# A decoder block on one core: two attention results in another PSUM pool, and three left operands of the last product prepared six steps ahead

## The chip, the cores and the metric

The kernel runs on one core of one Trainium2 chip. A core has a matrix engine (TensorE, PE in the profile), a vector engine (VectorE, DVE), an engine for activations and scaled copies (ScalarE, ACT), a general engine (GpSimd, POOL), and a queue that issues most transfers (SyncE, SP). Each runs its own list of instructions in order, and they wait for one another by semaphores. PE writes its results to PSUM, a small memory of banks that DVE and ACT can read. The metric is the time of one execution on the device, in microseconds.

## What is computed

One layer over 1024 tokens of width 1024, all in float32:

```python
def reference(x, ...):
    h = x
    h = h + 0.5 * swiglu(rms_norm(h, ffn1_norm), w1, w3, w2)       # width 2816
    u = rms_norm(h, mix_norm)
    proj = u @ w_in                                                # q | k | v | p | gates
    y_attn = dilated_mixture_attention(q, k, v) @ w_branch_attn    # 3 groups of 4 heads
    y_pool = multiscale_pool(pz, pool_w, pool_scale) @ w_branch_pool
    h = h + (gates[0] * y_attn + gates[1] * y_pool) @ w_out
    h = h + 0.5 * swiglu(rms_norm(h, ffn2_norm), w1, w3, w2)
    return rms_norm(h, final_norm)
```

In the attention each of the three groups has its own window and dilation; the group results of a head are added with weights that come from their softmax denominators.

## The kernel before

**Numbers in two parts.** Each float32 operand of a product is split into a high part, which ACT rounds off, and a low part, which DVE or POOL gets by subtracting the high part from the source. A product is then three matmuls: high by high, high by low, low by high. Large products are done as a scheme of seven block products in the place of eight, so sums and differences of blocks stand in front of the splits.

**The order of the work** is written out by hand: inside `tc.manual_schedule()` each engine runs its instructions in the order of the program text, and the tile framework only adds the waits. A tile is taken from a pool by its tag; each tag has a fixed number of places that are used in turn, and a new tile waits until the readers of the one that had its place before are done. PSUM has two tags of four places each, "mm" and "acc".

**The end of attention** (lines 1909 to 1943). The attention runs over 24 pairs of blocks, `q` from 0 to 23. For each pair `scores` makes the scores, DVE adds the mask (`masked`, line 1649), ACT takes exponents, `trans_p` has PE transpose them (`tp`), and `split_p` splits them into `ehi` (ACT) and `elo` (DVE, line 1693). `values(q)` has PE multiply them with the values, 12 matmuls of 256 columns into a PSUM place named `o` (line 1711), and `gather(q)` has DVE copy that to its rows in SBUF (line 1734). `next(fill)` places a piece of four matmuls of the pooling branch (`yp`, line 1770) between, so that PE has work while others prepare; two products of that branch, `yp14` and `yp15`, are still under way here. `scores` and the factor rows take "mm" places; `tp`, `o` and `yp` take "acc" places.

After the last pair come the factors of the second half of the heads: DVE computes `w` and `f` (lines 1582 to 1590), ACT and DVE spread them to `f_of` (lines 1598 and 1600, ACT for the first and third group), PE transposes them to `fa` (line 1609, "mm"), DVE multiplies the gathered rows with `fa` (line 1743), adds the three groups, with POOL (line 1745), and `att` is split by ACT and DVE (lines 1750 and 1751). Then `merge` has PE multiply `att` with the branch weights (`ya`, line 1836, "mm").

**The last product** (`Down`, lines 714 to 864). The down projection of each feed-forward half is seven products (`DOWN`) of six steps each (`PAIRS`), 42 steps, numbered 0 to 41; the name `f2` marks the second feed-forward half, with which the program ends. A step has a left operand, a block that was written to DRAM earlier, loaded by `load` as `g`, and a right operand, a weight block `raw` or the sum of two (`s_f2w`, line 790). `begin(i)` splits the right one into `bhi` and `blo` and the left one into `ahi` and `alo`, and frees weight blocks that are done with. `multiply` issues 24 matmuls of 512 columns for a step of two blocks (four groups of rows, six each) and 12 for the sixth step of a product, which has one block. `add` has DVE add a finished PSUM place to the rows `h` (`h_last`, line 820).

While step `i` is multiplied, the left operand of step `i + 3` is loaded and step `i + 2` is split. `split` gives the low part to DVE, or, for every fourth split outside the ends, to POOL, in halves of 512 columns:

```python
            self.n_lo += 1
            eng = gp if self.n_lo % 4 == 0 and 1 < n < self.last_shared else ve
```

`g` takes one of three places named `tmp`; `ahi`, `alo`, `bhi` and `blo` have three places each.

During steps 30 to 33 the first four rows of blocks are finished (`after2`, `norm_rows`): ACT squares a row, DVE and POOL get the scale (`nst`, lines 278 and 279), DVE writes the scaled row (`hn`, line 282), and SP sends it to DRAM (line 2234). In the last two steps, 40 and 41, the matmuls are ordered by row group: nine of a group, then its addition, then the end of the norm for the group's rows, which ACT, DVE and POOL share, and the transfers out.

## Time and profile before

| what | value |
|---|---|
| time, median of 3 runs (lowest to highest) | 1894.78 us (1894.72 to 1895.08) |
| the profiled execution, its own time | 1894.76 us |
| its span, first to last instruction | 1893.0 us |
| mean granted clock of TensorE | 0.999 |
| PE busy | 1880.3 us, 99% of the span |
| DVE, ACT, POOL busy | 1334.7, 773.2 and 713.3 us |

A row of the order of time has the start in microseconds from the span's start, the duration, the engine, the source line, the operation with its output and inputs (buffer numbers left out), the shapes, how many equal ones follow each other, and in brackets how long the engine had idled and what ended that. A row of waits has who waited for whom, the total, the number of times and the longest. A row of stretches has the busy time (and the number) of PE, PE's weight loads, DVE, ACT and POOL in it, PE's granted clock, the share of the DMA engines that was busy, and the rate in GB/s. Matmuls overlap: each is listed with some 0.39 us, but they start 0.23 us apart. Of PE's 12.7 us that are not busy, 7.8 lie behind the last matmul, at 1885.2.

### The profile page before, as it was taken

What the parts mean: (1) busy time and instruction counts of PE and PEld (TensorE: products, weight loads), DVE (VectorE), ACT (ScalarE), POOL (GpSimd) and SP (SyncE); (2) the same over time, 40 slices, a digit from 0 to 9 for tenths busy, and PEclk for the clock granted to TensorE, in tenths of its full rate; (3) what the DMA queues carried; (4) which work ended last, traced back from release to release, by engine and by line L of the source; (5) the groups of instructions that cost most, each with busy time, mean ns of one, the idle gap of its engine ahead of it and who ended that gap; (6) DMA issues with size and microseconds to landing.
All of it is one profiled execution on the core that took longest, in us unless ns stands there. A gap on an engine that the chain in (4) does not pass through costs nothing.

```text
span 1893.0 us, 24691 instructions
## 1 busy us (share of the span) xinstructions
PE 1880.3 (99%) x8822; PEld 1562.5 (83%) x8822; DVE 1334.7 (71%) x1975; ACT 773.2 (41%) x1394; POOL 713.3 (38%) x533
## 2 busy tenths in 40 slices
PE   9999999999999999999999999999999999999998
PEld 8888888888888888888888888888888888888886
DVE  6776556557786776657885896887665566577867
ACT  7423333333334543334445772363333333334344
POOL 4433333331223354444555457543333333312221
PEclk9999999999999999999999999999999999999999
DMA  5154223336566526765678868644332223354654
GB/s 191 60 196 167 84 89 108 138 113 214 169 227 207 183 86 210 234 223 195 214 244 314 322 222 287 266 151 153 141 126 99 88 102 118 132 197 157 224 194 145
DMA packets 144019, 330.79 MB, mean 175 GB/s; under 512 B 17560, under 2 KB 39064, under 8 KB 142360
## 3 DMA queue, kind: packets, MB, share of 16 engines
q1 hardware_dynamic: 140152, 318.36, 48.8%
q10 hardware_dynamic: 3744, 10.85, 1.6%
q8 instruction: 70, 1.15, 0.3%
q14 instruction: 53, 0.43, 0.1%
HBM read 229.61 MB, written 99.55 MB: 174 GB/s over the span
## 4 chain that ended last, share of the span: by engine, by line
PE 55%; DVE 2%; ACT 2%; issue 1%; POOL 0%; DMA 0%; ACTq 0%; SPq 0%; DVEq 0%; POOLq 0%
PE u_mixm L331 15%; PE d_f L815 8%; PE wo L2025 4%; PE yp L1770 2%; PE ya L1836 1%; PE o L1711 1%; PE u_f20b L331 1%; PE u_f21a L331 1%; PE u_f210b L331 1%; PE u_f210a L331 1%; PE u_f29b L331 1%; PE u_f29a L331 1%; PE u_f28b L331 1%; PE u_f28a L331 1%; PE u_f27b L331 1%; PE u_f27a L331 1%
## 5 line engine op out<-in xcount | busy, mean ns | idle before, releaser
L815 PE MATMUL d_f<-bhi_f,ahi_f 128*128 128x512 f32 x616 | 240.2, 390 | 0.0
L815 PE MATMUL d_f<-bhi_f,alo_f 128*128 128x512 f32 x616 | 239.8, 389 | 0.0
L815 PE MATMUL d_f<-blo_f,ahi_f 128*128 128x512 f32 x616 | 239.7, 389 | 0.0
L772 POOL TENSOR_TENSOR alo_f<-g_f,ahi_f 128x512 fp32r<-128x512 f32 x60 | 87.2, 1470 | 268.7 <-ACT ahi_f L768 268.7
L331 PE MATMUL u_mixm<-xhi_t_mix,wc_mixm 128*128 128x512 f32 x608 | 157.3, 391 | 0.1
L815 PEld LDWEIGHTS d_f<-bhi_f,ahi_f 128*128 128x128 f32 x616 | 115.7, 188 | 24.3 <-ACT h L415 0.4
L815 PEld LDWEIGHTS d_f<-bhi_f,alo_f 128*128 128x128 f32 x616 | 115.6, 188 | 24.2 <-DVE alo_f L772 0.4
L815 PEld LDWEIGHTS d_f<-blo_f,ahi_f 128*128 128x128 f32 x616 | 115.7, 188 | 23.9
L331 PEld LDWEIGHTS u_mixm<-xhi_t_mix,wc_mixm 128*128 128x128 f32 x608 | 113.5, 188 | 23.9 <-ACT wc_mixm L319 0.6
L331 PE MATMUL u_mixm<-xhi_b_mix,wc_mixm 128*128 128x512 f32 x456 | 120.4, 392 | 0.0
L322 POOL TENSOR_TENSOR wc_mixm<-s_mixm,wc_mixm 128x512 fp32r<-128x512 f32 x52 | 76.9, 1479 | 104.5 <-ACT wc_mixm L319 104.5
L331 PEld LDWEIGHTS u_mixm<-xhi_b_mix,wc_mixm 128*128 128x128 f32 x456 | 84.9, 188 | 17.5 <-issue 0.3
L319 ACT ACTIVATE wc_mixm<-s_mixm 128x512 fp32r<-128x512 f32 x76 | 47.0, 628 | 111.0 <-DVE s_mixm L373 54.0
L768 ACT ACTIVATE ahi_f<-g_f 128x1024 fp32r<-128x1024 f32 x84 | 81.9, 975 | 6.6 <-DMA g_f<-gs_f 6.6
L331 PE MATMUL u_mixm<-xlo_t_mix,wc_mixm 128*128 128x512 f32 x304 | 81.3, 389 | 0.0
L322 POOL TENSOR_TENSOR wc_mixm<-raw,wc_mixm 128x512 fp32r<-128x512 f32 x40 | 60.2, 1507 | 39.7 <-ACT wc_mixm L319 32.3
L2025 PE MATMUL wo<-w_o,o_hi 128*128 128x512 f32 x224 | 69.2, 391 | 0.0
L768 ACT ACTIVATE bhi_f<-s_f2w 128x512 fp32r<-128x512 f32 x55 | 32.9, 628 | 85.7 <-DVE s_f2w L790 67.0
L768 ACT ACTIVATE bhi_f<-s_f1w 128x512 fp32r<-128x512 f32 x55 | 33.0, 629 | 83.4 <-DVE s_f1w L790 70.1
L331 PEld LDWEIGHTS u_mixm<-xlo_t_mix,wc_mixm 128*128 128x128 f32 x304 | 57.1, 188 | 12.0
L772 DVE TENSOR_TENSOR alo_f<-g_f,ahi_f 128x1024 fp32r<-128x1024 f32 (+1 forms) x48 | 58.7, 1223 | 10.3 <-ACT ahi_f L768 10.3
L331 PE MATMUL u_mixm<-xlo_b_mix,wc_mixm 128*128 128x512 f32 x228 | 61.0, 389 | 0.0
(1332 smaller groups left out, 4754.5 us busy)
## 6 DMA issues: line engine op xcount, KB each, us to landing
g_f<-gs_f SPq DMA_DIRECT2D x70, 512.0 KB
gs_f<-y_f SPq DMA_DIRECT2D x88, 256.0 KB
raw<-in_w2a_dram SPq DMA_DIRECT2D x35, 512.0 KB
raw<-in_w2b_dram SPq DMA_DIRECT2D x35, 512.0 KB
gs_f<-gb_f SPq DMA_DIRECT2D x46, 256.0 KB
raw<-in_w1a_dram SPq DMA_DIRECT2D x22, 512.0 KB
raw<-in_w3a_dram SPq DMA_DIRECT2D x22, 512.0 KB
raw<-in_w1b_dram SPq DMA_DIRECT2D x22, 512.0 KB
```

The source lines that it names most:

```text
L319: ac.activation(w[:, 0], src, AF.Copy)
L322: eng.tensor_tensor(w[:, 1], src, w[:, 0].bitcast(F32), op=OP.subtract)
L331: pe.matmul(p, a, b, start=(start and n == 0), stop=(n == 11), skip_group_check=not start)
L768: ac.activation(hi[:, c], src, AF.Copy)
L772: eng.tensor_tensor(lo[:, d], src[:, o], hi[:, d].bitcast(F32), op=OP.subtract)
L815: pe.matmul(self.banks[m][t], l, r, start=(first and q == 0), stop=(last and q == 2))
L1711: pe.matmul(p, l, r, start=(j == 0), stop=(j == end))
L1770: pe.matmul(p, a, b, start=(j == 0), stop=(j == 11))
L1836: pe.matmul(p, a, b, start=(j == 0), stop=(j == 5))
L2025: pe.matmul(banks[m][t], l, r, start=(st == 0 and j == 0 and q == 0), stop=(st == 1 and j == 1 and q == 2))
```

## The change

Two places are changed; everything before 1130 us of the profile stands in the same order as before.

At the end of attention the last two results, `o22` and `o23`, take "mm" places; the split of the last pair is put ahead of the gathering of `o21`; and one piece of filling is moved from the first round of the final loop to the place ahead of it.

In the last product of the second feed-forward half, the left operands of steps 38, 39 and 40 are loaded seven steps ahead and split six steps ahead. They have two places of their own (`ge`), their low parts all go to POOL, and the rings of `ahi` and `alo` have six places.

```diff
@@ Down
+            self.early = range(len(self.steps) - 4, len(self.steps) - 1) if name == "f2" else ()
+            self.lefts = {}
...
         def split(self, side, srcs, n):
+            bufs = 6 if side == "a" and self.early else 3
...
-            self.n_lo += 1
-            eng = gp if self.n_lo % 4 == 0 and 1 < n < self.last_shared else ve
+            if side == "a" and n in self.early:
+                eng = gp
+            else:
+                self.n_lo += 1
+                eng = gp if self.n_lo % 4 == 0 and 1 < n < self.last_shared else ve
...
-            self.ops[i] = (self.split("a", [self.g.pop(i)], i), w)
+            if i not in self.lefts:
+                self.left(i)
+            self.ops[i] = (self.lefts.pop(i), w)
+
+        def left(self, i):
+            self.lefts[i] = self.split("a", [self.g.pop(i)], i)
+
+        def early_g(self, name):
+            return self.dp.tile([P, 1024], F32, tag="ge", bufs=2, name=name)
...
-                if i + 3 < n:
+                if i + 3 < n and i + 3 not in self.early:
                     self.load(i + 3)
+                if i + 7 in self.early:
+                    self.load(i + 7, self.early_g)
...
                 if i + 2 < n and not ahead:
                     self.begin(i + 2)
+                if i + 6 in self.early:
+                    self.left(i + 6)
@@ attention
-    def values(q):
-        both = outs[q] = bank("acc", f"o{q}")
+    def values(q, tag="acc"):
+        both = outs[q] = bank(tag, f"o{q}")
...
-        values(q - 2)
+        values(q - 2, "mm")
+        advance(splits[q - 1], 2)
         gather(q - 3)
-        advance(splits[q - 1], 2)
         advance(factors[1], 2)
         next(fill, None)
         end_branches()
-        values(q - 1)
+        values(q - 1, "mm")
         gather(q - 2)
         gather(q - 1)
+        next(fill, None)
         for n in range(8):
             advance(combines[1][n // 4])
-            if n not in (3, 5, 7):
+            if n not in (0, 3, 5, 7):
                 next(fill, None)
```

DVE's order behind the last pair, before (a name's first number is the pair, `o21` or `elo23`):

```order
L1582 TENSOR_TENSOR w1_10262<-top1_10261,stats1_8679 128x48
L1734 COPY o1_0_10208<-o21_10195 64x256 x2
L1693 TENSOR_TENSOR elo23_10288<-tp23_0_10251,ehi23_10287 128x512
L1693 TENSOR_TENSOR elo23_10288<-tp23_1_10252,ehi23_10287 128x512
L1586 TENSOR_TENSOR f1_10263<-w1_10262,stats1_8679 128x48
```

And now:

```order
L1600 TENSOR_TENSOR w1_10262<-top1_10261,stats1_8679 128x48
L1711 TENSOR_TENSOR elo23_10286<-tp23_0_10251,ehi23_10285 128x512
L1711 TENSOR_TENSOR elo23_10286<-tp23_1_10252,ehi23_10285 128x512
L1752 COPY o1_0_10208<-o21_10195 64x256 x2
L1604 TENSOR_TENSOR f1_10263<-w1_10262,stats1_8679 128x48
```

The copies of `o21` moved from ahead of the two subtractions to behind them; `f`, which follows both, stands where it stood.

PE's order at the same place, before, behind the matmuls of `o23`:

```order
L1609 MATMUL fa1_0_0_10324<-ident_70,f_of1_10299 128x128 x4
L1770 MATMUL yp14_10267<-xhi_t2_mix_5476,wab7_10015 128x512
L1770 MATMUL yp14_10267<-xlo_t2_mix_5477,wab7_10015 128x512 x3
L1609 MATMUL fa1_1_0_10335<-ident_70,f_of1_10299 128x128 x4
L1770 MATMUL yp15_10342<-xhi_b11_mix_3604,wab7_10015 128x512 x3
```

And now:

```order
L1788 MATMUL yp14_10267<-xhi_t2_mix_5476,wab7_10015 128x512
L1788 MATMUL yp14_10267<-xlo_t2_mix_5477,wab7_10015 128x512 x3
L1627 MATMUL fa1_0_0_10328<-ident_70,f_of1_10299 128x128 x4
L1627 MATMUL fa1_1_0_10335<-ident_70,f_of1_10299 128x128 x4
L1788 MATMUL yp15_10342<-xhi_b11_mix_3604,wab7_10015 128x512 x3
```

Four matmuls of the filling stand ahead of the first factor rows, no longer behind them.

POOL's order towards the end, before (`alo_f233` is the low part of step 33 of `f2`; `nst_2` and `nst_3` are the scales of the third and fourth row of blocks):

```order
L772 TENSOR_TENSOR alo_f233_15938<-g_f233_15889,ahi_f233_15937 128x512 x2
L279 TENSOR_TENSOR nst_2_15968<-nst_2_15968,mhalf_72 128x1
L279 TENSOR_TENSOR nst_3_16010<-nst_3_16010,mhalf_72 128x1
L772 TENSOR_TENSOR alo_f235_16023<-g_f235_15974,ahi_f235_16022 128x512
L2212 TENSOR_TENSOR nst_last4_16145<-nst_last4_16145,mhalf_72 128x1
```

And now:

```order
L778 TENSOR_TENSOR alo_f233_15940<-g_f233_15889,ahi_f233_15939 128x512 x2
L279 TENSOR_TENSOR nst_2_15970<-nst_2_15970,mhalf_72 128x1
L778 TENSOR_TENSOR alo_f238_15989<-g_f238_15933,ahi_f238_15988 128x512 x2
L279 TENSOR_TENSOR nst_3_16019<-nst_3_16019,mhalf_72 128x1
L778 TENSOR_TENSOR alo_f235_16034<-g_f235_15976,ahi_f235_16033 128x512
L778 TENSOR_TENSOR alo_f239_16038<-g_f239_15978,ahi_f239_16037 128x512 x2
L778 TENSOR_TENSOR alo_f240_16087<-g_f240_16027,ahi_f240_16086 128x512 x2
L2231 TENSOR_TENSOR nst_last4_16160<-nst_last4_16160,mhalf_72 128x1
```

The six halves of steps 38 to 40 are new on POOL, two of them ahead of `nst_3`. On ACT `ahi` 38 stands behind `ahi` 34, `ahi` 39 behind `ahi` 35, and `ahi` 40 between `ahi` 36 and the right operand of step 37. On SP load 38 stands behind load 34, load 39 behind load 35 and load 40 between the loads 36 and 37; load 40 waits until POOL is done with the first place of `ge`.

More of the change, by code (lines that the diff above doesn't have):

```diff
@@ L757, in split @@
         def split(self, side, srcs, n):
+            bufs = 6 if side == "a" and self.early else 3
             hi, lo = (
-                self.dp.tile([P, 2, HALF], F32R, tag=f"{side}{part}", bufs=3, name=f"{side}{part}_{self.name}{n}")
+                self.dp.tile([P, 2, HALF], F32R, tag=f"{side}{part}", bufs=bufs, name=f"{side}{part}_{self.name}{n}")
                 for part in ("hi", "lo")
             )
-            self.n_lo += 1
-            eng = gp if self.n_lo % 4 == 0 and 1 < n < self.last_shared else ve
+            if side == "a" and n in self.early:
[3 more added lines that the diff above has]
+                eng = gp if self.n_lo % 4 == 0 and 1 < n < self.last_shared else ve
             at = 0
```

## The prediction

> **What bounds the kernel now.** I read the totals first, then who waited for whom in the two stretches that the change touches (1120 to 1165 us, where attention ends, and 1839 to the end, the last product), and then the order of time there, engine by engine. The totals:
>
> ```profile
> PE 1880.3 (99%) x8822; PEld 1562.5 (83%) x8822; DVE 1334.7 (71%) x1975; ACT 773.2 (41%) x1394; POOL 713.3 (38%) x533
> ```
>
> PE is the bound: a gain is a stall of PE taken out, or a shorter tail behind its last matmul. The waits name one stall in each stretch (microseconds in total, times, longest):
>
> ```profile
> PE o L1711 <- DVE o L1734: 1.6, 1, 1.6
> ```
>
> ```profile
> PEld d_f L815 <- DVE alo_f L772: 0.4, 1, 0.4
> ```
>
> **Attention's end, before.** In order of time (start, duration, engine, line; in brackets the idle time ahead and what ended it):
>
> ```profile
> 1136.22 0.39 PE L1770 MATMUL yp<-xlo_b_mix,wab 128*128 128x512 f32 x1
> 1138.19 0.36 PE L1711 MATMUL o<-ehi,v_in 128*128 128x256 f32 x1 [1.57 <-DVE o L1734]
> ...
> 1140.62 0.28 PE L1711 MATMUL o<-ehi,v_in 128*128 128x256 f32 x1
> ...
> 1142.05 0.60 PE L1609 MATMUL fa<-ident,f_of 128*128 128x128 f32 x4
> 1142.41 0.48 PE L1770 MATMUL yp<-xhi_t_mix,wab 128*128 128x512 f32 x1
> ...
> 1143.42 0.60 PE L1609 MATMUL fa<-ident,f_of 128*128 128x128 f32 x4
> ...
> 1148.31 9.81 PE L1836 MATMUL ya<-att,ya 128*128 128x512 f32 x42
> ```
>
> ```profile
> 1137.19 0.85 DVE L1734 COPY o<-o 64x256 f32<-64x256 f32 x2
> 1138.38 1.29 DVE L1693 TENSOR_TENSOR elo<-tp,ehi 128x512 fp32r<-128x512 f32 x2 [0.34 <-ACT ehi L1690]
> 1139.59 0.20 DVE L1586 TENSOR_TENSOR f<-w,stats 128x48 f32<-128x48 f32 x1
> ...
> 1147.88 0.69 DVE L1751 TENSOR_TENSOR att<-o,att 128x512 fp32r<-128x512 f32 x1 [0.70 <-ACT att L1750]
> 1148.49 0.68 DVE L1743 TENSOR_TENSOR o<-o,fa 128x512 f32<-128x512 f32 x1
> ```
>
> ```profile
> 1140.77 2.00 ACT L1600 ACTIVATE f_of<-f 128x1024 f32<-128x1024 f32 x2 [1.80 <-DVE f L1590]
> ```
>
> The reader is to see three things. PE waits for the copy of gather 21 to free an "acc" place. DVE makes that copy in time in which it would otherwise wait for ACT's `ehi`. And behind it DVE runs one long chain (`elo`, the factors `f`, the copies, the products with `fa`, `att`) on which PE's `fa` and `ya` hang.
>
> **Term 1, attention's end.** One matmul of 512 columns takes 0.227 us ((1884.80 - 1878.67) / 27, from rows quoted below).
>
> - Removed: with `o22` in an "mm" place PE goes on at 1136.22 + 0.23 = 1136.45 instead of 1138.19: -1.74 us. The place's last reader, the masking of the last scores, stands ahead of `elo22` on DVE, and `o22` waits for that in any case.
> - `o23`: PE comes to it at 1136.45 + 2.43 (`o22` and half of `yp14`, 1138.19 to 1140.62) = 1138.88. It needs the first half of `elo23`, ready at 1138.38 + 0.65 = 1139.03, since DVE still waits for `ehi` there: +0.15.
> - The gathering is moved behind `elo23`. Its 0.85 us no longer lies in DVE's idle time (which grows from 0.34 to 1.19), so `f` starts at 1139.59 + 0.85 = 1140.44, and all that follows on DVE and ACT is 0.85 later.
> - `fa` of the first group needs ACT's first `f_of`: 1140.77 + 2.00 / 2 = 1141.77 before, 1142.62 now. PE is there at 1139.03 + 1.43 (`o23`) + 1.01 (the rest of `yp14`, which the extra filling puts ahead of it) = 1141.47: +1.15. The work done by 1142.98 was done by 1143.42 before, so PE is now 0.44 ahead.
> - `ya` needs `att`. PE is there at 1148.31 - 0.44 = 1147.87 and takes its low part with the fifth matmul, at 1148.78; DVE has it at 1147.88 + 0.61 + 0.85 = 1149.34: +0.6. PE is 0.15 behind the old times.
> - The second `ya` takes the place that DVE frees with the multiplication of 1148.49, now done at 1149.95. PE wants it at 1149.82: +0.1.
>
> Sum +0.3 us. Ends: -1.74, if nothing takes the wait's place; +0.85, if DVE's whole delay reaches PE. I take +0.3, because the rows give each link. From 1148 on PE stands without a gap for many steps, so I pass the shift on whole.
>
> **The last product, before.** DVE, then the helpers, then PE's end:
>
> ```profile
> 1842.71 0.69 DVE L820 SCALAR_TENSOR_TENSOR h_last<-d_f,h_last 128x512 f32<-128x512 f32 x1
> ...
> 1845.43 1.28 DVE L282 SCALAR_TENSOR_TENSOR hn_n<-h_last,nst,gain_final 128x1024 f32<-128x1024 f32 x1 [0.67 <-POOL nst L279]
> 1846.64 1.78 DVE L772 TENSOR_TENSOR blo_f<-raw,bhi_f 128x512 fp32r<-128x512 f32 x1
> ...
> 1854.10 1.23 DVE L772 TENSOR_TENSOR alo_f<-g_f,ahi_f 128x1024 fp32r<-128x1024 f32 x1 [3.01 <-ACT ahi_f L768]
> ...
> 1859.33 1.29 DVE L790 TENSOR_TENSOR s_f2w<-raw,raw 128x512 f32<-128x512 f32 x2
> ...
> 1862.26 1.23 DVE L772 TENSOR_TENSOR alo_f<-g_f,ahi_f 128x1024 fp32r<-128x1024 f32 x1 [0.18 <-ACT ahi_f L768]
> ...
> 1876.62 0.69 DVE L772 TENSOR_TENSOR blo_f<-s_f2w,bhi_f 128x512 fp32r<-128x512 f32 x1 [0.78 <-ACT bhi_f L768]
> ...
> 1880.23 0.69 DVE L820 SCALAR_TENSOR_TENSOR h_last<-d_f,h_last 128x512 f32<-128x512 f32 x1
> ...
> 1886.15 0.68 DVE L820 SCALAR_TENSOR_TENSOR h_last<-d_f,h_last 128x512 f32<-128x512 f32 x1
> ```
>
> ```profile
> 1839.77 1.06 ACT L768 ACTIVATE ahi_f<-g_f 128x1024 fp32r<-128x1024 f32 x1 [0.75 <-DMA g_f<-gs_f]
> 1843.43 1.06 ACT L274 ACTIVATE hn_n<-h_last 128x1024 f32<-128x1024 f32 x1 [2.59 <-DVE h_last L820]
> ...
> 1853.01 1.06 ACT L768 ACTIVATE ahi_f<-g_f 128x1024 fp32r<-128x1024 f32 x1 [2.72 <-DMA g_f<-gs_f]
> ```
>
> ```profile
> 1824.49 2.64 POOL L772 TENSOR_TENSOR alo_f<-g_f,ahi_f 128x512 fp32r<-128x512 f32 x2 [8.46 <-ACT ahi_f L768]
> ...
> 1835.05 3.65 POOL L772 TENSOR_TENSOR alo_f<-g_f,ahi_f 128x512 fp32r<-128x512 f32 x2 [1.22 <-ACT ahi_f L768]
> ...
> 1844.85 0.55 POOL L279 TENSOR_TENSOR nst<-nst,mhalf 128x1 f32<-128x1 f32 x1 [5.65 <-DVE nst L278]
> 1845.75 2.11 POOL L772 TENSOR_TENSOR alo_f<-g_f,ahi_f 128x512 fp32r<-128x512 f32 x1 [0.35 <-ACT ahi_f L768]
> ```
>
> ```profile
> 1835.68 0.32 SPq L754 DMA_DIRECT2D g_f<-gs_f  x1
> ...
> 1846.75 0.34 SPq L2234 DMA_DIRECT2D out_dram<-hn_n  x1
> 1847.19 1.20 SPq L754 DMA_DIRECT2D g_f<-gs_f  x2
> ```
>
> ```profile
> 1836.00:1839.50 3.50, 3.50 (x17) 2.92 (x16) 1.30 (x4) 2.10 (x3) 3.20 (x3) 1.00 0.85 300
> 1839.50:1841.00 1.50, 1.50 (x9) 1.23 (x8) 1.50 (x2) 1.06 (x1) 0.00 (x0) 1.00 0.00 0
> ```
>
> ```profile
> 1855.38 0.50 PE L815 MATMUL d_f<-bhi_f,alo_f 128*128 128x512 f32 x1
> ...
> 1878.67 0.39 PE L815 MATMUL d_f<-bhi_f,alo_f 128*128 128x512 f32 x1
> ...
> 1884.80 0.39 PE L815 MATMUL d_f<-bhi_f,alo_f 128*128 128x512 f32 x1
> ```
>
> PE hardly waits here: a few tenths at 1855.38, for the `alo` of step 36. What ends late is DVE: the first of the four last places was multiplied at 1878.67 + 0.39 = 1879.06 and added at 1880.23; the fourth was ready at 1885.19 and added at 1886.15, 0.96 late. DVE has gone without a real pause since 1854.10.
>
> **Term 2a, the tail.** The `alo` of steps 38, 39 and 40 leave DVE: three times 1.23 + 0.18, about 4 us, all ahead of 1880.23. The first last addition can then start when PE is done, and so, place by place (PE needs 9 x 0.227 = 2.04 us for each, DVE took (1886.15 - 1880.23) / 3 = 1.97), can the fourth: at 1885.25 and not 1886.15. What follows it is unchanged: -0.9 us. Ends: 0 and -0.96, since PE's end is not moved.
>
> **Term 2b, the front.** Six halves come to POOL, and three loads and three `ahi` come earlier.
>
> - Load 38 is issued behind load 34 (1835.68), about 1836.1. The DMA engines finish the two transfers ahead at 1839.3 and then idle until 1841, so half a megabyte at that stretch's 300 GB/s (1.75 us) lands by 1841.1 (estimate). ACT's `ahi` 38 takes 1.06, inside the 2.59 that it idled ahead of 1843.43.
> - POOL then makes `alo` 38 in 2.64 to 3.65 us, from 1842.3 to 1844.9 or 1845.9, and only then `nst` 3, which began at 1844.85. Behind `nst` 3 queue DVE's `hn` 3, its write on SP, load 36 behind that write, ACT's `ahi` 36, DVE's `alo` 36 and PE's step 36, which already waits. I take the shorter time, since DVE does little there but one addition out of PSUM: +0.3 with the hand-overs. Ends: 0 and +1.15.
> - `alo` 39 goes beside DVE's `blo` 35 and step 36's right operand. The row of 1846.64 shows the price of such company: 1.78 for a subtraction that takes 0.69 at 1876.62. DVE's 3.01 us of idle time at 1854.10 cover it; without them PE would wait at step 36.
> - `alo` 40 goes beside DVE's work for step 37, which PE reaches at 1855.4 + 24 x 0.227 = 1860.8. DVE had turned to the next step at 1859.33, 1.4 us earlier: covered, with little left.
> - Load 40 stands ahead of load 37 on SP's queue, so 37 lands one transfer (1.75 us) later. I take that as hidden under the sums and `blo` that step 37 needs first; at worst it is 1.75 - 1.4 = 0.35 us. The wider rings of `ahi` and `alo` cost nothing that I can see.
>
> The Trainium skill ("SBUF — State Buffer", section "Who interferes with whom") speaks against the move: a DVE instruction with two SBUF inputs and a GpSimd instruction that reads SBUF exclude each other, and the second to issue "**fully blocks**" for the first's whole duration. The trace agrees where POOL came late (2.64 grew to 3.65) and where DVE did (0.69 grew to 1.78). By it six halves of some 1.3 us could hold DVE up 7.9 us against 3.7 us of work saved, and the sum would be 4.2 us higher; by the rows most of that falls on DVE's idle time.
>
> **Sum.** +0.3 - 0.9 + 0.3 = -0.3 us. The profiled execution took 1894.76 us (span 1893.0, 1.76 around it), against a median of 1894.78: forecast 1894.5.
>
> **The rivals.**
>
> - The waits go and nothing replaces them: term 1 at -1.74, 2b at 0: 1894.76 - 1.74 - 0.9 = 1892.1. For it: the one named wait of PE, 1.57. Against it: DVE's chain, delayed 0.85, against slacks of 0.3 (`fa`) and 0.7 (`ya`). Chance 0.2.
> - Slower: load 38 lands late and `nst` 3 with it. Every microsecond after 1841.1 costs one; 0.9 eats the tail's gain. If it lands behind the write and load that follow, at 1844.5, `nst` 3 starts at 1844.5 + 1.06 + 2.64 = 1848.3, 3.4 late: 1894.76 + 0.3 - 0.9 + 3.4 = 1897.6, and with the longer POOL time 1898.6. Against it: the idle DMA row. Chance 0.13.
> - The tail does not gain, so that the second part does not do what it is made for: POOL's halves delay DVE as at 1846.64 (1.78 - 0.69 = 1.1 us each, three or four of the six), and that eats the 4 us taken off it. 2a at 0: 1894.76 + 0.6 = 1895.4. Against it: the 3.01 us in which DVE idles. Chance 0.16. If all six halves held DVE for their 1.32 us, behind its last pause, DVE would be 7.9 - 4 = 3.9 us later at the last addition: 1894.76 + 0.6 + 3.9 = 1899.3, chance 0.04. That is the skill's rule above carried to its end.
>
> **How the numbers follow.** The forecast's own case has 0.47, about 0.8 us either way. The range takes in the first and third rivals and leaves out most of the second: 1891.9 to 1896.2. About 0.2%, 3.8 us, is what a measurement of this kernel can tell from no change, so nearly all cases are "the same": slower than that takes the second rival at its worst (0.07), faster takes gains that no row here shows (0.04).
>
> **What would show it.** In the changed profile PE's wait for `o` is gone and waits of about 1 us for ACT's `f_of` and about half for `att` stand there, with `ya` starting within half a microsecond of 1148.3. The fourth last addition follows PE's last matmul by 0.1 and not 0.96. `nst` 3 starts near 1845.2. I am wrong if `ya` starts 1 us earlier, if `nst` 3 starts after 1846, or if any stretch outside these two moves.

## The result, and the profile after

The changed kernel takes 1897.19 us (median of 21 runs, 1896.08 to 1899.12), the kernel before 1894.1 us (21 runs, 1893.41 to 1895.22): ratio 1.0016, 95% interval 1.0010 to 1.0022. It is some 3 us slower, and lies above the forecast range. The profiled execution of the changed kernel took 1896.46 us (span 1894.3). The two profiles alone differ by 1.7 us only, because that of before lies 0.7 above the median of its 21 runs and that of the change 0.7 below its own; what the missing part is, the other kernels' profiles show below.

The totals of the changed kernel: PE is still busy nearly all the time, POOL works 9 us more.

```profile
PE 1880.9 (99%) x8822; PEld 1561.3 (82%) x8822; DVE 1335.9 (71%) x1972; ACT 773.2 (41%) x1394; POOL 722.6 (38%) x539
```

**Attention's end.** The changed kernel's order of time on PE, and then on DVE (columns as before: start, duration, engine, line, operation):

```profile
1136.26 0.28 PE L1729 MATMUL o<-ehi,v_in 128*128 128x256 f32 x1
...
1142.59 1.09 PE L1627 MATMUL fa<-ident,f_of 128*128 128x128 f32 x8 [1.13 <-ACT f_of L1618]
...
1147.99 1.26 PE L1854 MATMUL ya<-att,ya 128*128 128x512 f32 x4
1149.48 9.09 PE L1854 MATMUL ya<-att,ya 128*128 128x512 f32 x38 [0.23 <-DVE att L1769]
...
1159.93 0.50 PE L2044 MATMUL wo<-w_o,o_lo 128*128 128x512 f32 x1 [0.22 <-DVE o_lo L2032]
...
1164.36 4.02 PE L1854 MATMUL ya<-att,ya 128*128 128x512 f32 x17
```

```profile
1138.21 1.29 DVE L1711 TENSOR_TENSOR elo<-tp,ehi 128x512 fp32r<-128x512 f32 x2 [1.12 <-ACT ehi L1708]
1139.42 0.84 DVE L1752 COPY o<-o 64x256 f32<-64x256 f32 x2
1140.29 0.21 DVE L1604 TENSOR_TENSOR f<-w,stats 128x48 f32<-128x48 f32 x1
...
1148.73 0.69 DVE L1769 TENSOR_TENSOR att<-o,att 128x512 fp32r<-128x512 f32 x1 [0.70 <-ACT att L1768]
```

The wait of 1.57 for `o` is gone. DVE idles 1.12 ahead of `elo` and copies behind it, and PE stands 1.13 for `f_of`, 0.23 for `att` and, which the prediction did not have, 0.22 for `o_lo` of the output product.

**The last product.** The same kernel, DVE, then POOL, then PE:

```profile
1835.96 2.31 DVE L778 TENSOR_TENSOR blo_f<-raw,bhi_f 128x1024 fp32r<-128x1024 f32 x1
...
1847.42 2.33 DVE L282 SCALAR_TENSOR_TENSOR hn_n<-h_last,nst,gain_final 128x1024 f32<-128x1024 f32 x1 [0.98 <-POOL nst L279]
...
1851.37 2.38 DVE L796 TENSOR_TENSOR s_f2w<-raw,raw 128x512 f32<-128x512 f32 x2
...
1856.06 1.23 DVE L778 TENSOR_TENSOR alo_f<-g_f,ahi_f 128x1024 fp32r<-128x1024 f32 x1 [0.84 <-ACT ahi_f L774]
1857.20 2.39 DVE L796 TENSOR_TENSOR s_f2w<-raw,raw 128x512 f32<-128x512 f32 x2
1859.51 2.38 DVE L778 TENSOR_TENSOR blo_f<-s_f2w,bhi_f 128x512 fp32r<-128x512 f32 x2
1861.82 1.21 DVE L778 TENSOR_TENSOR alo_f<-g_f,ahi_f 128x1024 fp32r<-128x1024 f32 x1
...
1881.34 0.69 DVE L834 SCALAR_TENSOR_TENSOR h_last<-d_f,h_last 128x512 f32<-128x512 f32 x1 [1.61 <-PE d_f L829]
...
1887.46 0.69 DVE L834 SCALAR_TENSOR_TENSOR h_last<-d_f,h_last 128x512 f32<-128x512 f32 x1
```

```profile
1835.89 3.54 POOL L778 TENSOR_TENSOR alo_f<-g_f,ahi_f 128x512 fp32r<-128x512 f32 x2 [1.16 <-ACT ahi_f L774]
...
1843.37 3.50 POOL L778 TENSOR_TENSOR alo_f<-g_f,ahi_f 128x512 fp32r<-128x512 f32 x2 [2.49 <-ACT ahi_f L774]
1846.83 0.55 POOL L279 TENSOR_TENSOR nst<-nst,mhalf 128x1 f32<-128x1 f32 x1
1847.37 5.22 POOL L778 TENSOR_TENSOR alo_f<-g_f,ahi_f 128x512 fp32r<-128x512 f32 x3
1857.44 3.30 POOL L778 TENSOR_TENSOR alo_f<-g_f,ahi_f 128x512 fp32r<-128x512 f32 x2 [4.85 <-ACT ahi_f L774]
```

```profile
1856.08 0.49 PE L829 MATMUL d_f<-bhi_f,ahi_f 128*128 128x512 f32 x1 [0.23 <-ACT ahi_f L774]
1857.34 0.51 PE L829 MATMUL d_f<-bhi_f,alo_f 128*128 128x512 f32 x1 [0.53 <-DVE alo_f L778]
...
1863.09 0.50 PE L829 MATMUL d_f<-bhi_f,alo_f 128*128 128x512 f32 x1
...
1887.04 0.39 PE L829 MATMUL d_f<-bhi_f,alo_f 128*128 128x512 f32 x1
```

The additions at the end are on time, as forecast: DVE waits 1.61 for PE ahead of the first, and the fourth starts 0.42 behind the start of PE's last matmul (1.35 before). But PE itself is late. The first two of these rows are both of step 36, the third is of step 37. Counted by the starts of the matmuls, which are 0.23 apart without a wait, PE loses 1.31 at step 36 and 0.26 at step 37. Three pairs of DVE instructions that took 1.28 or 1.29 take 2.38 or 2.39, and hn 3 takes 2.33 in the place of 1.28, each beside a row of POOL's. The half beside hn 3, the first in the row of 1847.37, is that of `alo` 35, which is old work: before, it began 0.3 behind hn 3 and was the one held; now it stands in a row behind `alo` 38 and `nst` 3 and begins 0.05 ahead of hn 3.

Step 36 hangs on load 36, by the chain of work that ended last (start, duration, what):

```profile
1850.22 4.72 DMA g_f<-gs_f
1854.97 1.07 ACT ahi_f L774
```

From ACT's square of the second row of blocks ("row 1", 1832.76 here and 1831.87 before) to this load it is 17.46, and it was 15.32 before (1847.19): 2.1 more. Of that, 0.8 come from `blo` 34, which takes 2.31 and not 1.22 (the last section tells why), 0.3 from POOL's queue ahead of `nst` 3, and 1.05 from hn 3.

**Three stretches.** Times since the start of the span carry whatever happened earlier in that run, so I compare lengths, one profiled execution of each kernel. Stretch I runs from the first `fa` rows of 1134 to the second block of `ya` on PE; stretch II from ACT's square of row 1 to PE's last matmul; stretch III from that matmul to the issue of ACT's last transfer. In the kernel before, the first two marks of PE and the mark of ACT are

```profile
1134.21 0.60 PE L1609 MATMUL fa<-ident,f_of 128*128 128x128 f32 x4
...
1163.44 4.92 PE L1836 MATMUL ya<-att,ya 128*128 128x512 f32 x21
```

```profile
1831.87 1.06 ACT L274 ACTIVATE hn_n<-h_last 128x1024 f32<-128x1024 f32 x1 [3.46 <-DVE h_last L820]
```

so I is 1163.44 - 1134.21 = 29.23 and II is 1884.80 - 1831.87 = 52.93. From the same rows of each profiled execution, with the times of all kernels (each beside runs of the kernel before on its own chip):

| kernel | median us | before there | ratio, 95% interval | I | II | III |
|---|---|---|---|---|---|---|
| before | 1894.1 | | | 29.23 | 52.93 | 4.78 |
| the change | 1897.19 | 1894.1 | 1.0016 (1.0010 to 1.0022) | 30.34 | 54.28 | 3.66 |
| the change, again | 1896.76 | 1894.35 | 1.0013 (1.0004 to 1.0022) | 30.26 | 54.52 | 3.66 |
| attention's edits alone | 1895.3 | 1893.97 | 1.0004 (0.9995 to 1.0013) | 30.26 | 52.62 | 3.88 |
| the two places alone | 1893.6 | 1893.97 | 0.9998 (0.9989 to 1.0007) | 29.14 | 52.62 | 4.01 |
| places and filling | 1894.11 | 1894.02 | 1.0001 (0.9992 to 1.0010) | 29.34 | 52.62 | 3.68 |
| last product's edits alone | 1895.88 | 1893.97 | 1.0009 (1.0000 to 1.0018) | 29.20 | 54.02 | 3.68 |
| the same, low parts on DVE | 1894.81 | 1893.97 | 1.0003 (0.9995 to 1.0012) | 29.21 | 53.78 | 3.68 |
| steps 39 and 40, on DVE | 1894.38 | 1894.02 | 1.0002 (0.9994 to 1.0011) | 29.19 | 53.46 | 3.66 |
| steps 39 and 40, on POOL | 1894.79 | 1894.02 | 1.0004 (0.9995 to 1.0013) | 29.21 | 53.87 | 3.68 |
| before, loads first | 1893.57 | 1894.02 | 1.0000 (0.9991 to 1.0009) | 29.18 | 52.62 | 3.67 |
| the change, loads first | 1896.96 | 1894.35 | 1.0015 (1.0006 to 1.0024) | 30.26 | 54.95 | 3.66 |
| on DVE, loads first | 1894.19 | 1893.91 | 1.0001 (0.9992 to 1.0011) | 29.20 | 53.10 | 3.66 |
| steps 39, 40 on POOL, loads first | 1894.75 | 1893.91 | 1.0004 (0.9995 to 1.0014) | 29.22 | 53.87 | 3.66 |
| places, loads first | 1893.49 | 1894.35 | 0.9998 (0.9989 to 1.0007) | 29.17 | 52.63 | 3.66 |
| the same, `ehi` first | 1893.55 | 1894.35 | 0.9997 (0.9988 to 1.0006) | 29.64 | 52.62 | 3.66 |

Most of the intervals are some 1.7 us to either side, wider than most of these edits, so the times by themselves tell little; the stretches tell more. Stretch I is 29.18 to 29.23 in all eight kernels with the old end of attention, and II is 52.62 or 52.63 in six kernels, with the old order of splits: that is PE without a wait. The seventh kernel with them is the one before itself, with 52.93. So in six of the seven profiles the old code loses nothing in II, and the change loses 1.0 to 1.1 in I and 1.7 to 1.9 in II. The new last product is less steady than that: the same code gave 54.02, 54.28 and 54.52, so that a difference of a few tenths in II between two of its kernels means little by itself.

### The profile page after: what moved, and what is told of

It is laid out like the page before. It is cut to its first block, busy times and chain, and to the rows that moved or that the text cites. A ratio compares the mean times of both kernels' runs of the same rounds, so it can differ in the third digit from the quotient of the medians.

```text
span 1894.3 us, 24664 instructions
## 1 busy us (share of the span) xinstructions
PE 1880.9 (99%) x8822; PEld 1561.3 (82%) x8822; DVE 1335.9 (71%) x1972; ACT 773.2 (41%) x1394; POOL 722.6 (38%) x539
## 3 DMA queue, kind: packets, MB, share of 16 engines
q8 instruction: 70, 1.15, 0.2%
## 4 chain that ended last, share of the span: by engine, by line
PE 55%; DVE 2%; DMA 1%; ACT 1%; issue 1%; POOL 1%; SPq 0%; ACTq 0%; DVEq 0%
PE u_mixm L331 15%; PE d_f L829 9%; PE wo L2044 4%; PE yp L1788 1%; PE u_f20b L331 1%; PE u_f21a L331 1%; PE u_f210b L331 1%; PE u_f210a L331 1%; PE u_f29b L331 1%; PE u_f29a L331 1%; PE u_f28b L331 1%; PE u_f28a L331 1%; PE u_f27b L331 1%; PE u_f27a L331 1%; PE u_f26b L331 1%; PE u_f26a L331 1%
## 5 line engine op out<-in xcount | busy, mean ns | idle before, releaser
L778 POOL TENSOR_TENSOR alo_f<-g_f,ahi_f 128x512 fp32r<-128x512 f32 x66 | 95.7, 1467 | 277.0 <-ACT ahi_f L774 277.0
L774 ACT ACTIVATE ahi_f<-g_f 128x1024 fp32r<-128x1024 f32 (+1 forms) x84 | 81.9, 975 | 2.7 <-DMA g_f<-gs_f 2.7
L778 DVE TENSOR_TENSOR alo_f<-g_f,ahi_f 128x1024 fp32r<-128x1024 f32 (+1 forms) x45 | 53.9, 1198 | 6.5 <-ACT ahi_f L774 6.5
```

The source lines that it names most:

```text
L774: ac.activation(hi[:, c], src, AF.Copy)
L778: eng.tensor_tensor(lo[:, d], src[:, o], hi[:, d].bitcast(F32), op=OP.subtract)
```

## The experiments

### Attention: which of its three edits costs

The kernel before with attention's three edits:

```diff
...
-        values(q - 2)
+        values(q - 2, "mm")
+        advance(splits[q - 1], 2)
         gather(q - 3)
-        advance(splits[q - 1], 2)
...
-        values(q - 1)
+        values(q - 1, "mm")
...
+        next(fill, None)
...
-            if n not in (3, 5, 7):
+            if n not in (0, 3, 5, 7):
```

> Attention's edits alone; the last product is that of before. Theory A, from the two profiles: the wait of 1.57 us for the place of `o` goes, and DVE's chain, 0.85 later, takes it back and more (PE waits 1.1 for `f_of`, and some 1.5 in short waits for `att` and for `o_lo` of the output product). PE starts the last product about 1 us later than before, and the time is 1.0 us above before (0.7 to 1.3). Rival B, my working on record: the chain takes back all but little of it, +0.3 (0 to 0.6).

Measured: 1895.3 against 1893.97, +1.3, and I is 1.03 longer than before. The waits are those of the whole change; its PE and the waits of PE's weight loads:

```profile
1142.51 1.09 PE L1609 MATMUL fa<-ident,f_of 128*128 128x128 f32 x8 [1.14 <-ACT f_of L1600]
```

```profile
PEld fa L1609 <- ACT f_of L1600: 1.6, 1, 1.6
PEld wo L2026 <- DVE o_lo L2014: 0.6, 1, 0.6
PEld ya L1836 <- DVE att L1751: 0.5, 1, 0.5
```

Theory A holds, at the upper end of its time. Then the two places alone:

```diff
-    def values(q):
-        both = outs[q] = bank("acc", f"o{q}")
+    def values(q, tag="acc"):
+        both = outs[q] = bank(tag, f"o{q}")
...
-        values(q - 2)
+        values(q - 2, "mm")
         gather(q - 3)
         advance(splits[q - 1], 2)
...
-        values(q - 1)
+        values(q - 1, "mm")
```

> The two `mm` places alone: `o21` is gathered ahead of the split of the last pair, and the filling stands, both as before. Theory A (the moved gathering is what costs): `f`, `att` and `o_lo` come as early as before, PE waits about 1.3 us for `f_of` in the place of 1.57 for the place of `o`, and the waits for `att` and `o_lo` are not there: 0.3 to 0.7 us under before. Rival B (the places are what costs, because `fa` and `ya` want them): the waits of about 1.5 us for `att` and `o_lo` stay and the time is 0.5 to 1 us above before.

Measured: 1893.6 against 1893.97; I is 29.14, 0.09 under before. PE, in the order of time:

```profile
1141.57 0.66 PE L1609 MATMUL fa<-ident,f_of 128*128 128x128 f32 x4 [1.19 <-ACT f_of L1600]
```

The wait of 1.57 was worth 0.09: a wait for `f_of` stood right behind it, unseen in the profile of before because PE came late to it, and `fa` starts only 0.15 earlier (7.69 and not 7.84 behind the first mark). The places do no harm. The medians differ by 0.37, inside A's range, but the stretch shows only 0.09 of it: the sign is A's, the gain smaller than A said. The third kernel adds the moved filling and leaves the gathering where it was:

```diff
         gather(q - 1)
+        next(fill, None)
         for n in range(8):
             advance(combines[1][n // 4])
-            if n not in (3, 5, 7):
+            if n not in (0, 3, 5, 7):
```

> The two `mm` places and the moved filling, with `o21` gathered ahead of the split as in the kernel before. Theory A (the moved gathering is the whole cost of attention's edits): the four matmuls of filling lie in PE's wait for `f_of`, which falls from 1.19 to about 0.3 us; PE reaches `ya` some 0.9 earlier and gives 0.2 to 0.5 of that back to `att` and `o_lo`: 0.5 to 0.8 us under before. Rival B (`att` and `o_lo` set the pace whatever PE does ahead of them): what is saved at `f_of` is waited out there, and the time is that with the places alone, 0.1 to 0.4 under before.

Measured: 1894.11 against 1894.02, I 29.34. PE's wait for `f_of` falls from 1.19 to 0.24, as A said, but the time comes back at `att` (0.20) and at the output product:

```profile
1159.12 0.50 PE L2026 MATMUL wo<-w_o,o_lo 128*128 128x512 f32 x1 [0.25 <-DVE o_lo L2014]
```

Rival B holds, with 0.2 us to the worse: DVE's chain sets the pace, whatever PE does ahead of it. This kernel differs from attention's edits alone in the place of the gathering only, and its I is 0.92 shorter (30.26 - 29.34): the 0.85 us of copies that left DVE's idle time, and no other edit, are what attention's part costs.

### The last product: alone, and without POOL

The change with the old end of attention:

```diff
-        values(q - 2, "mm")
-        advance(splits[q - 1], 2)
+        values(q - 2)
         gather(q - 3)
+        advance(splits[q - 1], 2)
...
-        values(q - 1, "mm")
+        values(q - 1)
```

> The last product's edits alone; attention is that of before. Theory A (POOL's halves and DVE slow each other, POOL stands ahead of the scale `nst` 3, and what is left of it reaches PE at steps 36 and 37): PE's last matmul ends 1.3 us or more later than before, the tail is 0.9 shorter, the time 0.4 to 2 us above before, and by how much changes from run to run with which of the two engines is held. Rival B, my working on record: +0.3 and -0.9, so 0.6 us under before.

Measured: 1895.88 against 1893.97, +1.9; II is 54.02, 1.40 over 52.62 (1.09 over the 52.93 of before, where A had said 1.3 or more). PE waits at steps 36 and 37 as in the whole change, 1.03 and 0.28 by the starts of its matmuls. 0.6 of the 1.9 lies outside the span (2.40 against 1.78 in the median). The 1.3 and 1.9 of the two halves alone make 3.2; the whole cost 3.1 in one set of runs and 2.4 in another. Theory A's time and waits hold. Then the low parts on DVE, in the same places:

```diff
             if side == "a" and n in self.early:
-                eng = gp
+                eng = ve
```

> The last product's edits alone, with the three early low parts on DVE in the place of POOL; loads and high parts stand as in the change. Theory A (POOL's company is the cost): `alo` 38 delays the addition ahead of `nst` 3 by 1.14 us on DVE, and that delay alone is handed on to step 36; DVE's instructions keep their undisturbed times (hn 3 1.28, `s_f2w` 0.69 each), step 37 is in time. +1.14 - 0.9, so 0.2 us above before (-0.2 to +0.5). Theory B (the order of the transfers: loads 38 and 39 ahead of load 36 and load 40 ahead of 37 is the cost): load 36 lands as late as in the change, steps 36 and 37 wait as there, and the time is within 0.3 us of that of the last product's edits alone with POOL.

Measured: 1894.81 against 1893.97, II 53.78. The median is 1.1 us under that with POOL, but 0.6 of that lies outside the span (1.78 against 2.40), and II is only 0.24 shorter. Step 37 is in time, as A said, so POOL's company costs there; step 36 waits as long as with POOL (1.07 against 1.03), more than A allowed. `nst` 3 is 1.9 late: 1.14 by `alo` 38 ahead of it on DVE, as A said, and 0.8 by the race at `blo` 34 that the section on the hardware tells; the kernel with POOL was spared that. At step 36, then, this pair does not tell A from B. Next, step 38 is left out:

```diff
-            self.early = range(len(self.steps) - 4, len(self.steps) - 1) if name == "f2" else ()
+            self.early = range(len(self.steps) - 3, len(self.steps) - 1) if name == "f2" else ()
```

> The last product's edits for steps 39 and 40 alone, with their low parts on DVE; step 38 is loaded and split as in the kernel before. Theory A (the cost of the change lies in step 38 ahead of `nst` 3 and in POOL's company): `nst` 3 starts on time, hn 3 takes 1.28, steps 36 and 37 are in time and the fourth last addition is on time: 0 to 0.8 us under before. Rival B (load 39 ahead of load 36 and load 40 ahead of 37 cost by themselves): load 36 lands later than in the kernel before by a transfer's 1.7 us, PE waits for `ahi` and `alo` at step 36, 0.4 us or more above before.

> As the kernel with steps 39 and 40 alone, with their low parts on POOL. Theory A1 (company at step 37 costs by itself): `nst` 3 and hn 3 are on time, but POOL's two halves of step 40 stretch `s_f2w` and `blo` of step 37 to 2.38 us each as in the change, and PE waits about 1 us there: 0.3 to 1 us above before. Theory A2 (only POOL ahead of `nst` 3 and the late hn 3 cost; with DVE that much earlier, the company is covered): 0 to 0.8 us under before, as with DVE.

Measured: on DVE 1894.38 against 1894.02, II 53.46, PE waiting 0.5 at step 36; on POOL 1894.79, II 53.87, waiting 0.5 at step 37, where `s_f2w` and `blo` are stretched. A1's time and wait hold for POOL. On DVE neither A nor B is met as written: load 36 landed 21.6 behind the square of row 1, where it was 21.0 before and 19.8 in the profile of attention's edits alone, so some of B may be in it. In both kernels `nst` 3 was itself 0.8 late, for a reason that no theory had and that the section on the hardware tells (the race at `blo` 34).

### The load of step 36

In the kernel before I now took load 36 for the weak place: it is issued behind the write of hn 3, and DVE's pause ahead of `alo` 36 is the wait for it. The load goes ahead of the addition and the norm:

```diff
             for i, (m, s) in enumerate(self.steps):
...
+                if self.name == "f2" and i + 3 < n:
+                    self.load(i + 3)
                 ahead = tick is None and m == len(DOWN) - 1 and i + 2 < n
...
-                if i + 3 < n:
+                if self.name != "f2" and i + 3 < n:
                     self.load(i + 3)
```

> The kernel before with one move on SP's queue: in the last product the load of step i + 3 is issued ahead of the addition and the norm of step i, so load 36 no longer stands behind the write of hn 3. Theory A (in the kernel before, what makes the last additions late is load 36, which is issued behind that write and lands late): load 36 lands before 1848, DVE's pause ahead of `alo` 36 (1.8 to 3.0 us) shrinks, PE's wait of 0.4 for it goes, and the fourth last addition starts when PE is done: 0.2 to 0.8 us under before. Rival B (it is DVE's sheer work that makes them late): the pause is gone but the additions are as late as before and the time is the same, within 0.2 us.

Measured: 1893.57 against 1894.02, II 52.62, III 3.67. DVE goes from `blo` to `alo` 36 without the long pause, and starts it 19.40 behind the square of row 1, where the kernel before started it at 22.23 (1854.10 - 1831.87):

```profile
1851.01 1.23 DVE L772 TENSOR_TENSOR alo_f<-g_f,ahi_f 128x1024 fp32r<-128x1024 f32 x1 [0.18 <-ACT ahi_f L768]
```

By the stretches A holds: the wait at step 36 and the late additions are gone. The time moved by 0.45, inside its interval. But kernels with the old last product untouched show nearly the same II and III (52.62, and 3.68 to 4.01). The reason stands in the chains of work that ended last, first of the kernel before, then of attention's edits alone (start, duration, what):

```profile
1847.19 5.72 DMA g_f<-gs_f
1853.01 1.07 ACT ahi_f L768
1854.10 1.23 DVE alo_f L772
```

```profile
1847.94 4.48 DMA g_f<-gs_f
1852.52 1.07 ACT ahi_f L768
1853.62 1.23 DVE alo_f L772
```

The same load took 5.72 in the one profile and 4.48 in the other, and the chain runs on from it through DVE to the last additions in both. So the 0.96 that the fourth addition was late belongs to the execution that was profiled. Why the load took longer there, no run shows. Then the same move in the whole change:

> The whole change, with one move more on SP's queue: in the last product the loads of step i + 3 are issued ahead of the addition and the norm of step i, so load 36 does not stand behind the write of hn 3. Theory A (what the last product's edits cost reaches PE through one chain: `nst` 3, hn 3, its write, load 36, `ahi` and `alo` 36): POOL is as late and DVE's instructions are as stretched as in the change, but load 36 lands before 1848, PE's wait at step 36 goes, and PE's stretch from the square of row 1 to the last matmul falls by 1.0 to 1.7 us; what is left over the kernel before is attention's 1.0 and what the time outside the span adds: 0.8 to 1.8 us above before. Rival B (POOL's company at step 37 costs by itself): PE still waits a microsecond or more at step 37 and the time is 2.3 us or more above before.

> The change, unaltered, beside the kernel above on the same chip and for a second look at its order of time. Theory A: 2.5 to 3.5 us above before; PE waits at steps 36 and 37 again, for a sum of 1.2 to 1.8 us, and how much of it stands at which step goes with whether POOL or DVE is the one held at `alo` 33 and `blo` 34. Rival: the waits of the first profile were a chance of that run, and the sum is under 0.8 here.

Measured, side by side: 1896.96 with the load first, 1896.76 without. The theory that the load's chain is the only way to PE falls: II gets longer, not shorter. Load 36 is there in time, and PE waits at both steps all the same, for ACT and DVE, which POOL holds up; by the starts of the matmuls it loses 1.45 at step 36 and 0.79 at step 37. Rival B's time is met (2.6 above), its wait at step 37 nearly. DVE, then PE, of the change with the loads first:

```profile
1843.27 2.31 DVE L778 TENSOR_TENSOR alo_f<-g_f,ahi_f 128x1024 fp32r<-128x1024 f32 x1
...
1851.13 3.47 DVE L796 TENSOR_TENSOR s_f2w<-raw,raw 128x512 f32<-128x512 f32 x2
...
1857.39 3.48 DVE L796 TENSOR_TENSOR s_f2w<-raw,raw 128x512 f32<-128x512 f32 x2
```

```profile
1857.52 0.50 PE L829 MATMUL d_f<-bhi_f,alo_f 128*128 128x512 f32 x1 [0.53 <-DVE alo_f L778]
...
1863.79 0.50 PE L829 MATMUL d_f<-bhi_f,alo_f 128*128 128x512 f32 x1 [0.52 <-DVE alo_f L778]
```

Now five of POOL's six new halves hold DVE: 1.09 at `alo` 34 (2.31 - 1.22), 2.19 and 2.20 at the two `s_f2w` pairs, 5.5 us in all. In the first profile of the change it was 1.05 at hn 3 and 1.1 at each of three pairs, 4.3 us, of which some 0.5 took the place of short waits for ACT that stood there before. The three low parts that DVE was spared take 3 x 1.23 = 3.7. The second profile of the change repeats the first: II is 54.52, and PE loses 1.56 at step 36 and 0.26 at step 37, about as its theory A said; the time, 2.4 above before, is just under A's 2.5.

That left two questions: is POOL's company enough by itself, and could DVE do the work with the load early? Both kernels take the change's last product with the loads first and the old end of attention, one with the low parts on DVE, one with steps 39 and 40 alone on POOL:

```diff
-            self.early = range(len(self.steps) - 4, len(self.steps) - 1) if name == "f2" else ()
+            self.early = range(len(self.steps) - 3, len(self.steps) - 1) if name == "f2" else ()
...
+                if self.name == "f2" and i + 3 < n and i + 3 not in self.early:
+                    self.load(i + 3)
                 ahead = tick is None and m == len(DOWN) - 1 and i + 2 < n
...
-                if i + 3 < n and i + 3 not in self.early:
+                if self.name != "f2" and i + 3 < n:
                     self.load(i + 3)
```

This is the one with steps 39 and 40; the other keeps the range of the change and has `eng = ve`.

> The last product's edits with the three early low parts on DVE, and the loads of step i + 3 issued ahead of the addition and the norm of step i. Theory C (POOL's company and the late load 36 each hold DVE's `alo` 36 back by itself; either is enough): with neither, PE waits at neither step 36 nor 37, and its stretch from the square of row 1 to the last matmul is within 0.2 us of the 52.62 that it takes without a wait; time 0.5 us under to 0.2 above before. Rival D (three more low parts ahead of step 37 are too much for DVE wherever they run): PE waits 0.5 us or more at step 36 or 37.

> The last product's edits for steps 39 and 40 alone, low parts on POOL, and the loads of step i + 3 issued ahead of the addition and the norm of step i. Theory C: POOL's company alone holds DVE back: `s_f2w` and `blo` of steps 36 and 37 are stretched together by 2 us or more, PE waits 0.5 to 1.3 us at step 37, and the time is 0.5 to 1.2 us above before. Rival E (what is left without step 38 was the load): no wait of PE above 0.2 us, the time 0 to 0.5 us under before.

Measured: on DVE 1894.19 against 1893.91, II 53.10, with one short wait, at step 36; on POOL 1894.75, II 53.87, the same as with the late load. PE's rows, first on DVE, then on POOL:

```profile
1855.83 0.50 PE L829 MATMUL d_f<-bhi_f,alo_f 128*128 128x512 f32 x1 [0.18 <-DVE alo_f L778]
```

```profile
1861.78 0.50 PE L829 MATMUL d_f<-bhi_f,alo_f 128*128 128x512 f32 x1 [0.54 <-DVE alo_f L778]
```

Theory C holds for POOL: without a late load it still costs 1.25, and moving the load changes nothing of it. On DVE the early load takes 0.68 of 1.16 away; the 0.48 left is over C's 0.2, and the wait of 0.18 is under D's 0.5, so neither is met. Whether the 0.48 comes of three more low parts or of the race at `blo` 34, which held DVE in this run too, is not shown. The two kernels here are the plainest pair on POOL's price: both have the loads first and both were held at `blo` 34, and two low parts on POOL cost PE 1.25 where three on DVE cost 0.48.

### Two attempts at a faster kernel

The first kernel has the places and the loads first. The second has also ACT's `ehi` of the last pair ahead of the split of `att`, with all three gatherings behind `f_of`; its edit against the first:

```diff
-        advance(combines[0][1], 2)
+        advance(combines[0][1])
         trans_p(q - 1)
         splits[q - 1] = split_p(q - 1)
+        advance(splits[q - 1])
+        advance(combines[0][1])
         advance(factors[1])
         next(fill, None)
         values(q - 2, "mm")
-        gather(q - 3)
-        advance(splits[q - 1], 2)
+        advance(splits[q - 1])
         advance(factors[1], 2)
...
         values(q - 1, "mm")
+        gather(q - 3)
         gather(q - 2)
```

> The kernel before with the two `mm` places (nothing else of the change) and the early issue of the loads of the last product. By the single runs: 0.1 from the places, 0.3 from step 36, 0 to 0.9 from the tail, less some 0.4 that the time outside the span was longer with the moved loads: 0.2 to 0.8 us under before. If the gains of the two do not add, it is within 0.2 us of the kernel with the moved loads alone.

> As the kernel with places and loads, and at the end of attention ACT's `ehi` of the last pair stands ahead of the split of `att`, for which ACT waits on POOL, and `o21` is gathered behind the copy of `f_of` with the two others. Theory A (DVE's chain sets the pace there, and it starts at `ehi`): DVE goes on to `elo` without a pause, `f` comes 1 us earlier, PE's wait for `f_of` goes, but DVE has no idle time left and PE gives most of that back at `att` and `o_lo`: the output product starts 0.3 to 0.6 us earlier than with the places and loads alone. Rival B (the moved copies delay the products with `fa` as they did in the change): no gain or up to 0.5 us later.

Measured: 1893.49 and 1893.55 against 1894.35 on the same chip. Their medians are the lowest of all, and neither can be told from the kernel before by its interval (0.9998 and 0.9997). The first is 0.86 under before, just past what was expected. In the second, I is 0.47 longer: rival B. DVE does go on to `elo` without a pause, but `f` is done only 0.5 earlier, counted from the first mark of stretch I, since its first instruction now runs beside POOL's half of `att` (1137.80 to 1139.10) and takes 0.92, where it took 0.20:

```profile
1138.24 0.92 DVE L1588 TENSOR_TENSOR f<-w,stats 128x48 f32<-128x48 f32 x1
```

And the copies behind `f_of` delay the products with `fa` as in the change, here by 0.4.

## Why the prediction was wrong

- **Term 1, +0.3; measured +1.0 to +1.1** (stretch I). The links were right as far as they were drawn: the wait for `o` gone, `f_of` waited for 1.13 (1.15 forecast), `ya` held by `att`. The step that failed is "I pass the shift on whole". DVE stays 1.0 (at `att`) to 1.4 (at `o_lo`) behind, counted from the first mark, and PE's slack ahead of the output product is smaller than that: the waits for `o_lo` add 0.47 (by the same count the `wo` block ends 1.11 late, having begun 0.64 late). Another 0.3 is PE being less far ahead at `ya` than forecast: 0.13 and not 0.44.
- **Term 2a, -0.9.** The additions do start with PE's end, so the mechanism is right, and between the two profiles III falls by 1.12. As a saving over the kernel before it is wrong: III there is 3.68 to 4.01 in the profiles of other kernels with that last product, so the typical gain is 0 to 0.35. The failed step is the first one, that the lateness seen in one execution is always there. It came of a load that took 5.72 and not 4.48.
- **Term 2b, +0.3; measured +1.4 between the profiles, +1.7 to 1.9 against PE without a wait.** `nst` 3 began at 1846.83, past the 1846 that the prediction had named as a sign of being wrong. Counted from the square of row 1 it was 1.1 late: 0.3 by POOL's queue, as forecast (0.54 behind DVE's `nst` where it was 0.24), and 0.8 by the race at `blo` 34, which no term had. That the 0.3 came out is partly luck: `alo` 38 took 3.50 and not the 2.64 of the sum, and the late DVE hid that. In the second profile DVE was not late, load 38 landed 0.7 later, and POOL's queue cost 0.6. The failed steps are the two covers. DVE's pause of 3.01 was no free time: it was the wait for load 36, which hangs on `nst` 3 and hn 3, so it moved along with them and had shrunk to 0.84 when it came. Load 36 was issued 2.1 later, half of that because POOL held hn 3, which the prediction did not foresee, and PE lost 1.3 at step 36. And the 1.4 ahead of step 37 was gone by then, so that the company of `alo` 40 (2.2 us on `s_f2w` and `blo`) met PE, which lost 0.3 there. With the load early PE lost even more, to POOL's company and the race (II 54.95). The price of one company, 1.1, stood in the prediction, and the sum counted none of it.
- **The rivals.** The last of them, in which the halves of POOL hold DVE for as long as they run, with 1899.3 and a chance of 0.04, was nearest in its mechanism. What it had wrong is the place: the delay falls on PE's steps 36 and 37, not on the last additions. The second rival's 1897.6 is nearest in number, but by luck: its cause, load 38 landing 3.4 late, did not happen (counted from the square of row 1 it landed 0.2 behind the estimate, and 0.8 in the second profile). Its sum has a slip, 1848.3 for 1848.2, that changes nothing. The Trainium skill ("SBUF — State Buffer", section "Who interferes with whom") says that the two exclude each other, and the trace agrees in kind: DVE's instructions became 4.3 and 5.5 us longer, of the 6 x 1.3 that POOL's halves take.
- **The rest.** Attention's 1.1, 1.7 to 1.9 in the last product, and up to 0.35 of gain in the tail make 2.5 to 3.0. The time outside the span, which the prediction left as it was, adds 0.3 to 0.4 (2.15 against 1.78 to 1.83, medians of the runs). Together that is 2.8 to 3.4; measured were 3.1, which the two profiles alone hid, and 2.4 in the second set of runs. "Any stretch outside these two moves" did not happen: from the end of I to the start of II it is 668.4 in both.

## What to carry to other kernels

Before you count a stall as a gain, find what is late next on the same engine: here 1.57 us of waiting were worth 0.1 at most, since a chain on DVE stood right behind. Idle time of a helper that is itself waiting for a long chain is no cover for work that lengthens this chain. And work that was moved to POOL beside a DVE with two inputs in SBUF was paid here with DVE's time, instruction by instruction: 4.3 and 5.5 us for 3.7 us of work. That is not unloading at all.

## What the runs showed of the hardware

**A race at `blo` 34.** At `alo` 33 on POOL and `blo` 34 on DVE the two start almost together. In all seven kernels with the old splits POOL starts 0.01 or 0.02 earlier by the trace, DVE takes 1.22 and POOL 3.65 for its two halves. In seven of the nine profiles with early low parts POOL starts 0.07 or 0.08 earlier (in the first profile of the change at 1835.89 and 1835.96, in the kernel before at 1835.05 and 1835.07), and then DVE takes 2.31 and POOL 3.54. The other two, the second profile of the change and the last product's edits alone, go as with the old splits, so the same kernel has gone both ways. DVE's delay is handed on to its part of `nst` 3, 0.8 us; it did not decide II, which was longer in the profile of the change without it (54.52 against 54.28). The Trainium skill ("SBUF — State Buffer", section "Who interferes with whom") says that the order of issue decides who is held. The trace agrees where POOL is 0.07 ahead; where it is 0.01 or 0.02 ahead by its recorded start, it is POOL that is held, so either these starts are not the order of issue to some hundredths or something else decides, which no run shows. Why POOL comes 0.05 earlier in some profiles, I have not found.

**The time outside the span differs from kernel to kernel.** It is 1.74 to 1.88 in some kernels, run after run (attention's edits alone, the last kernel above), and 2.1 to 2.3 in others (the change, the change with the loads first). The last product's edits alone have 2.1 to 3.1, and the kernel before is mostly at 1.8 and in some runs over 2, up to 3.7. Its length does not go with either half of the change: the kernel before with nothing but its loads moved has 2.17 in the median, and the last product's edits with the low parts on DVE have 1.78. What sets it is open.
